# Two of the four weight sums of a column group, made by accumulating transfers from GpSimd's queue instead of VectorE adds

## The chip, the cores and the metric

The kernel runs on one core of a Trainium2 chip. The metric is the device time of one execution in microseconds (us). TensorE is called PE, VectorE DVE, ScalarE ACT, GpSimd POOL, and SyncE's queue, from which the kernel of before issues all its transfers, SP.

## What is computed

One decoder layer on a 1024 x 1024 float32 input: an RMSNorm, one input projection with a 1024 x 6144 weight, two token mixers side by side on its columns (retention with eight heads; a gated linear recurrence of width 1024), an output projection, the residual sum and a second RMSNorm.

```
xn = rms_norm(x, norm_in_g)
q, k, v, g_ret, x_lru, g_lru = split(xn @ w_in)           # six times 1024 columns
y_ret = group_norm(retention(rotary(q), rotary(k), v)) * silu(g_ret)
y_lru = rg_lru(conv(x_lru), gates) * silu(g_lru)
out   = rms_norm(x + concat(y_ret, y_lru) @ w_out, norm_out_g)
```

This case is about the product `xn @ w_in` for the 5120 columns other than v.

## The kernel before

**The product.** A float32 product is made of three products of rounded parts: a matrix is split into a high part (a cast on ACT, line 106) and a low part (a subtraction on DVE, line 107), and `mm3` (line 109) multiplies high by high, low by high and high by low. Above that stands a scheme with seven products in place of eight. The input is cut into four quarters (whose sums, P1 to P7, are made once, in the v stage, and kept), and so are 256 columns of the weight: `b11`, `b12` (upper 512 rows, first and second half of the columns), `b21`, `b22` (lower 512 rows). A **column group** (class `Quad`, line 383) is such a set of 256 columns; there are 20, here numbered 0 to 19. Groups 0 to 11 are the columns of x_lru, g_lru and g_ret, three groups for each pair of recurrence blocks; groups 12 to 19 are q and k, whose columns lie in the order (h j c) (`halves=True`).

**The sums of a group.** The seven products need four sums of weight quarters. `t13[:, 0]` is b11 + b12 (used by P5), `t13[:, 1]` is b12 + b22 (P7), `t24[:, 0]` is `t13[:, 0]` + b22 (P6) and `t24[:, 1]` is `t24[:, 0]` + b21 (P4). All four are DVE adds of 128 x 512 elements: lines 415, 434, 416 and 426. `t13` and `t24` are tiles of 128 x 1024 from the pool `sums`, which has two buffers; a third user is `graw`, the gate weights of a pair of recurrence blocks (line 628), once in three of the groups 0 to 11.

**The preparation of a group.** `load` (line 391) asks SP for the raw weight, two transfers of 512 KB. `prep1` splits b11 for P1 and makes `t13[:, 0]` and `t24[:, 0]`; `prep2` splits b21 and b22 (P2, P3) and makes `t24[:, 1]`; `prep3` splits `t24` (P6, P4) and makes `t13[:, 1]`; `prep4` splits `t13` (P5, P7). The split of `t24` and that of `t13` are an ACT cast and a DVE subtraction of 128 x 1024 each.

**What sets the order.** `Runner.step` (line 500) interleaves the products of one group with the preparation of the next and with pieces of the work behind the product (convolution, gates, scan, rotation), which are called fillers. A scheduler then places the instructions of each engine in a fixed order by dependences and its own costs; each engine runs its instructions strictly in that order, and one that waits holds up all that stand behind it on that engine. A tile takes the buffer of its pool that was released first. Twelve matmuls make one of the seven products of a group.

**Gates.** The recurrence's gates are matmuls with `gw` (line 591), the split form of `graw`. They stand between the products of the groups, and PE can't start them before `graw` has landed and been split.

Of the kernel before, what the change touches and what calls it, by code (L numbers as in the profile page):

```python
# [10 lines left out]
F32 = mybir.dt.float32  # L11
# [3 lines left out]
ALU = mybir.AluOpType  # L15

P = 128
# [23 lines left out]
def hybrid_layer(  # L41
# [17 lines left out]
    pe, act, dve, pool, sp = nc.tensor, nc.scalar, nc.vector, nc.gpsimd, nc.sync  # L59
# [3 lines left out]
    HALF = D // 2  # L63
# [3 lines left out]
    def pool_on(side, name, bufs):  # L67
        return tc.tile_pool(name=name, bufs=bufs, side=side, reuse_waits="tile")
# [36 lines left out]
    def split(src, hi, lo):  # L105
        act.copy(out=hi, in_=src)  # L106
        dve.tensor_tensor(out=lo, in0=src, in1=hi.bitcast(F32), op=ALU.subtract)  # L107
# [57 lines left out]
    sums = s_stack.enter_context(pool_on("right", "sums", 2))  # L165
# [83 lines left out]
    def v_phase():  # L249
        with pool_on("left", "vb", 6) as vb, pool_on("left", "vo", 10) as vo:  # L250
# [52 lines left out]
            for k in range(4):  # L303
                for t in range(4):
                    product("P1", A[t], t, True, False, [k])
            b21 = load(1, 0, vb, "bt")
            load_x("A12", xs_pool["P4"], "w", 1, 0)
            w_parts("P2", b21)
            x_parts("P2", xr["A12"])
            for t in range(4):  # L310
                snap("c11", t, A[t])
            load_x("A21", xs_pool["P4"], "w", 0, 1)
            b12 = load(0, 1, vb, "bt")
            load_x("A22", sums, "sum", 1, 1)
            b22 = load(1, 1, raw, "raw")

            combine(b11, b11, b12, ALU.add)
# [65 lines left out]
    class Quad:  # L383
# [7 lines left out]
        def load(self):  # L391
            r = raw.tile([P, 8, 256], F32, name="wraw", tag="raw")
            for kh in range(2):
                sp.dma_start(out=r[:, 4 * kh:4 * kh + 4],
                             in_=w_in[kh * HALF:(kh + 1) * HALF, self.col:self.col + 256]
                             .rearrange("(k p) c -> p k c", p=P))
            b = r.rearrange(self.order, kh=2, j=2, h=2)
            self.b = [[b[:, kh, :, j] for j in range(2)] for kh in range(2)]
            self.w = {}

        def pair(self):
            return [slabs.tile([P, 2, 4, 2, 64], F32R, name="wq", tag="w") for _ in range(2)]
# [5 lines left out]
        def prep1(self):  # L408
            (b11, b12), (b21, b22) = self.b
            s = slabs.tile([P, 2, 4, 2, 64], F32R, name="w11", tag="w")  # L410
            split(b11, s[:, 0], s[:, 1])
            self.put("P1", s[:, 0], s[:, 1])
            self.t24 = sums.tile([P, 2, 4, 2, 64], F32, name="t24", tag="sum")
            self.t13 = sums.tile([P, 2, 4, 2, 64], F32, name="t13", tag="sum")
            dve.tensor_tensor(out=self.t13[:, 0], in0=b11, in1=b12, op=ALU.add)
            dve.tensor_tensor(out=self.t24[:, 0], in0=self.t13[:, 0], in1=b22, op=ALU.add)

        def prep2(self):
# [9 lines left out]
        def prep3(self):  # L428
            (b11, b12), (b21, b22) = self.b
            h, l = self.pair()  # L430
            split(self.t24, h, l)
            self.put("P6", h[:, 0], l[:, 0])
            self.put("P4", h[:, 1], l[:, 1])
            dve.tensor_tensor(out=self.t13[:, 1], in0=b12, in1=b22, op=ALU.add)

        def prep4(self):
            h, l = self.pair()
# [257 lines left out]
    while run.i < len(run.q):  # L695
# [3 lines left out]
    op = {n: ctx.enter_context(pool_on("right", n, k)) for n, k in (  # L699
        ("qkc", 4), ("wraw", 3), ("wo", 10), ("yl", 16), ("vc", 4), ("h", 8))}  # L700
# [316 lines left out]
```

## Time and profile before

| | |
|---|---|
| median of 3 runs (lowest to highest) | 767.24 us (765.67 to 769.76) |
| the profiled execution: its own time, its span | 765.5 us, 763.7 us |
| PE busy, DVE busy, ACT busy, POOL busy | 734.1 us (96%), 548.6 us (72%), 413.4 us (54%), 0.2 us |
| granted TensorE clock, mean | 0.993 |
| stretch of the 20 column groups | from 89.7 us to 494.3 us of the span |

A row of the timeline gives the start and the length of an instruction in us, its engine and line, what it writes and reads, and in brackets how long its engine sat idle before it and what ended that. Consecutive instructions of an engine overlap a little, so the distance of two starts is less than a length. A matmul's row is longer than the distance to the next one, since matmuls are pipelined.

### The profile page before, as it was taken

Reading aid. Unit: us, or ns where it says so; the run is one execution under the profiler, and the core shown is the slowest. Engines: PE = TensorE matmul, PEld = TensorE weight load, DVE = VectorE, ACT = ScalarE, POOL = GpSimd, SP = SyncE. Lnnn points to the kernel's source line nnn. Section 1 sums busy time; section 2 is a strip of 40 time slices with the busy share of each in tenths; the row PEclk is TensorE's granted clock in tenths of the full one; section 3 lists DMA queues with packets and bytes.
Section 4 is the critical chain, followed back from the end, with each engine's and each line's share of the span. In section 5 each row is a group of like instructions: output and inputs, shape, how many; then the busy total and the mean of one; then the engine's idle time right before and its main releaser. Section 6 shows DMA issues by size and latency. Waiting matters only on the chain.

```text
span 763.7 us, 9411 instructions
## 1 busy us (share of the span) xinstructions
PE 734.1 (96%) x3508; PEld 610.8 (80%) x3508; DVE 548.6 (72%) x918; ACT 413.4 (54%) x635; POOL 0.2 (0%) x4
## 2 busy tenths in 40 slices
PE   6999999999999999999999999968999999899996
PEld 5877888887787788788788888757888898788885
DVE  6998647669977968977899888585567665652443
ACT  7784436695599679679533333255435443431332
POOL 0000000000000000000000000000000000000000
PEclk9999999999999999999999999999999999999999
DMA  9752712141214212421445542789946556331022
GB/s 317 268 191 88 245 53 70 56 128 38 72 52 161 74 55 87 148 83 52 169 122 126 134 110 56 226 266 323 313 146 206 194 179 235 97 129 36 28 88 106
DMA packets 85406, 105.58 MB, mean 138 GB/s; under 512 B 4848, under 2 KB 58224, under 8 KB 85360
## 3 DMA queue, kind: packets, MB, share of 16 engines
q1 hardware_dynamic: 85360, 104.99, 43.0%
q8 instruction: 27, 0.44, 0.2%
q14 instruction: 19, 0.16, 0.1%
HBM read 75.61 MB, written 29.36 MB: 137 GB/s over the span
## 4 chain that ended last, share of the span: by engine, by line
PE 67%; DVE 13%; ACT 10%; DMA 5%; issue 4%; SPq 0%; DVEq 0%; ACTq 0%
PE pp L112 59%; PE pp L826 2%; DVE xc L561 2%; PE pp L825 2%; PE pp L808 2%; PE pp L787 2%; DMA yraw<-l_d 2%; DVE wq L107 1%; ACT wq L106 1%; PE pp L847 1%; DVE y L614 1%; DVE wl L107 1%; DMA rot<-in_rot_t 1%; ACT L643 1%; PE pp L794 1%
## 5 line engine op out<-in xcount | busy, mean ns | idle before, releaser
L112 PE MATMUL pp<-wh,wq 128*128 128x512 f32 x960 | 301.6, 391 | 1.6 <-ACT cy L470 0.7
L112 PEld LDWEIGHTS pp<-wh,wq 128*128 128x128 f32 x960 | 179.9, 188 | 42.9 <-ACT cy L461 2.2
L112 PE MATMUL pp<-wo,yt 128*128 128x512 f32 (+1 forms) x792 | 186.1, 390 | 3.9 <-ACT yt L106 3.9
L112 PE MATMUL pp<-wl,wq 128*128 128x512 f32 x480 | 186.9, 389 | 0.0
L112 PEld LDWEIGHTS pp<-wo,yt 128*128 128x128 f32 x792 | 143.4, 189 | 31.6 <-ACT yt L106 4.3
L112 PEld LDWEIGHTS pp<-wl,wq 128*128 128x128 f32 x480 | 90.1, 188 | 18.5
L107 DVE TENSOR_TENSOR wq<-t,wq 128x1024 fp32r<-128x1024 f32 x40 | 48.7, 1221 | 39.1 <-ACT wq L106 32.1
L106 ACT CAST wq<-t 128x1024 fp32r<-128x1024 f32 x40 | 41.7, 1049 | 31.3 <-PE pp L112 26.7
L112 PE MATMUL pp<-wh 128*128 128x512 f32 x112 | 45.6, 407 | 8.0 <-ACT wh L106 8.0
L112 PE MATMUL pp<-wh,w 128*128 128x512 f32 x160 | 52.9, 391 | 0.1
L112 PE MATMUL pp<-wl,wh 128*128 128x512 f32 x112 | 44.8, 401 | 0.0
L112 PE MATMUL pp<-wh,wl 128*128 128x512 f32 x112 | 44.1, 398 | 0.0
L898 ACT ACTIVATE junk<-h 128x512 f32<-128x512 f32 (+1 forms) x17 | 10.3, 607 | 49.8 <-DVE h L914 25.3
L461 ACT COPY cy<-pp 128x512 f32<-128x512 f32 x20 | 11.6, 581 | 46.1 <-PE pp L112 45.5
L112 PEld LDWEIGHTS pp<-wh,w 128*128 128x128 f32 x160 | 30.0, 188 | 6.9 <-DVE w L107 0.6
L112 PEld LDWEIGHTS pp<-wh 128*128 128x128 f32 x112 | 21.8, 195 | 13.2 <-ACT wh L106 8.4
L112 PE MATMUL pp<-wl,w 128*128 128x512 f32 x80 | 31.1, 389 | 0.0
L839 ACT ACTIVATE yn<-pp,nb,rs_y 128x128 f32<-128x128 f32 x64 | 24.1, 458 | 11.8 <-DVE nb L837 11.8
L470 ACT COPY cy<-pp 128x512 f32<-128x512 f32 x20 | 11.6, 578 | 29.4 <-PE pp L112 29.3
L422 ACT CAST wq<-wraw 128x512 fp32r<-128x512 f32 x40 | 22.9, 617 | 8.3 <-PE pp L112 7.4
L97 ACT ACTIVATE rs_s<-ve 128x4 f32<-128x4 f32 x16 | 3.2, 202 | 43.8 <-DVE ve L832 43.8
L424 DVE TENSOR_TENSOR wq<-wraw,wq 128x512 fp32r<-128x512 f32 x40 | 26.7, 681 | 0.1
(154 smaller groups left out, 1116.2 us busy)
## 6 DMA issues: line engine op xcount, KB each, us to landing
wraw<-in_w_in SPq DMA_DIRECT2D x40, 512.0 KB, 4.7
qkc<-qk_d SPq DMA_DIRECT2D x16, 512.0 KB, 5.1
wor<-in_w_out SPq DMA_DIRECT2D x16, 512.0 KB, 5.7
bt<-in_w_in SPq DMA_DIRECT2D x20, 256.0 KB, 5.4
xA<-in_xT SPq DMA_DIRECT2D x16, 256.0 KB, 5.4
v_d<-vo SPq DMA_DIRECT2D x16, 256.0 KB, 2.4
xt<-in_x SPq DMA_DIRECT2D x8, 512.0 KB, 3.3
l_d<-y SPq DMA_DIRECT2D x8, 512.0 KB, 3.2
```

What stands on the lines that cost most here:

```text
L106: act.copy(out=hi, in_=src)
L107: dve.tensor_tensor(out=lo, in0=src, in1=hi.bitcast(F32), op=ALU.subtract)
L112: pe.matmul(ps, a, b, start=first and j == 0, stop=last and j == 2, skip_group_check=True)
L422: act.copy(out=h[:, j], in_=b)
L424: dve.tensor_tensor(out=l[:, j], in0=b, in1=h[:, j].bitcast(F32), op=ALU.subtract)
L461: act.copy(out=self.cy[:, :TH], in_=self.A)
L561: dve.scalar_tensor_tensor(out=xc[:, d:], in0=c[:, :T - d], scalar=cw[3 - d], in1=xc[:, d:], op0=ALU.mult, op1=ALU.add)
L787: heads(lambda h, hs: pe.matmul(psc[:, hs], k[:, hs], q[:, hs], start=True, stop=True))
L808: heads(lambda h, hs: pe.matmul(pkv[:, hs], kn[:, hs], vn[:, hs], start=True, stop=True))
L825: pe.matmul(po[:, hs], q[:, hs], st[:, h], start=True, stop=False)
L826: pe.matmul(po[:, hs], sm[:, h], vn[:, hs], start=st is None, stop=True)
L839: heads(lambda h, hs: act.activation(out=yn[:, hs], in_=po[:, hs], func=AF.Identity, scale=rs[:, h:h + 1], bias=nb[:, h:h + 1]))
```

## The change

`load` now also takes a buffer for `t13` and fills it by transfers. SP copies b11 into `t13[:, 0]` and b12 into `t13[:, 1]` straight from the weight in HBM (256 KB each; one transfer each in groups 0 to 11, two of 128 KB each in groups 12 to 19, where a row of 128 columns is two pieces of 64). Then POOL's queue issues transfers that read the weight again and add it to what stands in SBUF (`accum_op`): b12 onto `t13[:, 0]`, b22 onto `t13[:, 1]`. These are cut along k, so a group has four of 128 KB in groups 0 to 11 and eight of 64 KB in groups 12 to 19. A POOL transfer waits for SP's transfer into the same bytes, and DVE's add of `t24[:, 0]` (now line 431) waits for those of `t13[:, 0]`. The two DVE adds of `t13` are gone, 40 instructions in all. Nothing else is edited, but the scheduler orders all engines anew, and lines behind 416 move by 15 or 14: 426 is now 441, 424 is 439, 457 is 471, 471 is 485, 480 is 494, 543 is 557, 561 is 575, 613 is 627, 669 and 670 are 683 and 684, 678 and 679 are 692 and 693.

```diff
             self.b = [[b[:, kh, :, j] for j in range(2)] for kh in range(2)]
             self.w = {}
+            self.t13 = sums.tile([P, 2, 4, 2, 64], F32, name="t13", tag="sum")
+            for j, (kh0, kh1) in enumerate(((0, 0), (0, 1))):
+                for kh, jj, o in ((kh0, j, None), (kh1, 1, ALU.add)):
+                    src = w_in[kh * HALF:(kh + 1) * HALF, self.col:self.col + 256] \
+                        .rearrange(self.order.replace("p (kh k)", "(k p)").replace("kh ", ""), p=P, j=2, h=2)[:, :, jj]
+                    if self.order.endswith("(h j c) -> p kh k j h c"):
+                        for h in range(2):
+                            if o is None:
+                                sp.dma_start(out=self.t13[:, j, :, h], in_=src[:, :, h])
+                            else:
+                                for k in (0, 2):
+                                    pool.dma_start(out=self.t13[:, j, k:k + 2, h], in_=src[:, k:k + 2, h], accum_op=o)
+                    elif o is None:
+                        sp.dma_start(out=self.t13[:, j].rearrange("p k h c -> p k (h c)"), in_=src.rearrange("p k h c -> p k (h c)"))
+                    else:
+                        for k in (0, 2):
+                            pool.dma_start(out=self.t13[:, j, k:k + 2].rearrange("p k h c -> p k (h c)"), in_=src[:, k:k + 2].rearrange("p k h c -> p k (h c)"), accum_op=o)
...
             self.t24 = sums.tile([P, 2, 4, 2, 64], F32, name="t24", tag="sum")
-            self.t13 = sums.tile([P, 2, 4, 2, 64], F32, name="t13", tag="sum")
-            dve.tensor_tensor(out=self.t13[:, 0], in0=b11, in1=b12, op=ALU.add)
             dve.tensor_tensor(out=self.t24[:, 0], in0=self.t13[:, 0], in1=b22, op=ALU.add)
...
             self.put("P4", h[:, 1], l[:, 1])
-            dve.tensor_tensor(out=self.t13[:, 1], in0=b12, in1=b22, op=ALU.add)
```

**Which buffer `t13` takes.** In the program that results, `t13` of a group takes the buffer of the group before's `t24`, which DVE releases by its split of that `t24`; in groups 3, 6, 9 and 12, where `graw` took that one, it takes the buffer of the group before's `t13`.

**DVE, the preparation of group 4.** In these rows a tile's number tells its buffer. Before, `t24_1199` and `t13_1200` are group 3's, `t24_1358`, `t13_1359` and `w11_1355` are group 4's. Before, on DVE from group 3's split of `t24` to group 4's second add of `t24`:

```order
L107 TENSOR_TENSOR wq_1277<-t24_1199,wq_1276 128x1024
L415 TENSOR_TENSOR t13_1359<-wraw_1323 128x512
L434 TENSOR_TENSOR t13_1359<-wraw_1323 128x512
L543 TENSOR_TENSOR cx_1082<-cx_1082,rstd_b_71 128x1024
L480 TENSOR_TENSOR cy_1083<-pp_1203,cy_1083 128x512
L107 TENSOR_TENSOR wq_1318<-t13_1200,wq_1317 128x1024
L107 TENSOR_TENSOR w11_1355<-wraw_1323,w11_1355 128x512
L416 TENSOR_TENSOR t24_1358<-t13_1359,wraw_1323 128x512
L457 TENSOR_TENSOR cx_1260<-pp_1326,cx_1260 128x512
L426 TENSOR_TENSOR t24_1358<-t24_1358,wraw_1323 128x512
```

and now, where `t24_1218` and `t13_1177` are group 3's, `t13_1342`, `t24_1381` and `w11_1378` are group 4's:

```order
L107 TENSOR_TENSOR wq_1294<-t24_1218,wq_1293 128x1024
L485 TENSOR_TENSOR cy_1096<-pp_1220,cy_1096 128x512
L607 TENSOR_TENSOR y_1255<-y_1255,xc_1116 128x1024
L107 TENSOR_TENSOR wq_1334<-t13_1177,wq_1333 128x1024
L431 TENSOR_TENSOR t24_1381<-t13_1342,wraw_1339 128x512
L441 TENSOR_TENSOR t24_1381<-t24_1381,wraw_1339 128x512
L557 TENSOR_TENSOR cx_1095<-cx_1095,rstd_b_71 128x1024
L494 TENSOR_TENSOR cy_1096<-pp_1220,cy_1096 128x512
L107 TENSOR_TENSOR w11_1378<-wraw_1339,w11_1378 128x512
```

The add of line 431 needs the transfers into `t13_1342`, which may start when the split of `t24_1218` has released that buffer. The low part of P1's weight (`w11`), which stood ahead of the first add of `t24`, now stands four instructions behind it.

**PE, the gates between groups 3 to 5.** `gw` is the gates' weight, `xh` their input; `wh_429`, `wh_430`, `wl_431`, `wl_432` belong to P6. Before, from the first matmul of P6 of group 5 to the first gate:

```order
L112 MATMUL pp_1549<-wh_429,wq_1563 128x512
L112 MATMUL pp_1549<-wl_431,wq_1563 128x512
L112 MATMUL pp_1549<-wh_429,wq_1564 128x512
L112 MATMUL pp_1549<-wh_429,wq_1563 128x512
L112 MATMUL pp_1549<-wl_431,wq_1563 128x512
L112 MATMUL pp_1549<-wh_429,wq_1564 128x512
L112 MATMUL pp_1549<-wh_430,wq_1563 128x512
L112 MATMUL pp_1549<-wl_432,wq_1563 128x512
L112 MATMUL pp_1549<-wh_430,wq_1564 128x512
L112 MATMUL pp_1549<-wh_430,wq_1563 128x512
L112 MATMUL pp_1549<-wl_432,wq_1563 128x512
L112 MATMUL pp_1587<-xh_1517,gw_1544 128x512
```

and now, the same stretch:

```order
L112 MATMUL pp_1574<-wh_429,wq_1588 128x512
L112 MATMUL pp_1574<-wl_431,wq_1588 128x512
L112 MATMUL pp_1574<-wh_429,wq_1589 128x512
L112 MATMUL pp_1611<-xh_1542,gw_1569 128x512
```

The first gate stood behind eleven matmuls of P6 and now stands behind three. In the next pair of blocks (group 8) it stood behind eight matmuls of P6 and now stands behind one; in the last (group 11) behind one, and now behind three.

**DVE, a q/k group (18).** Before, from group 17's split of `t24` (`t24_3435`) to group 18's second add of `t24` (`t24_3569`; `t13_3570` and `w11_3566` are its own):

```order
L107 TENSOR_TENSOR wq_3498<-t24_3435,wq_3497 128x1024
L471 TENSOR_TENSOR cy_3348<-pp_3443,cy_3348 128x512
L415 TENSOR_TENSOR t13_3570<-wraw_3532 128x512
L434 TENSOR_TENSOR t13_3570<-wraw_3532 128x512
L107 TENSOR_TENSOR wq_3529<-t13_3436,wq_3528 128x1024
L416 TENSOR_TENSOR t24_3569<-t13_3570,wraw_3532 128x512
L107 TENSOR_TENSOR w11_3566<-wraw_3532,w11_3566 128x512
L426 TENSOR_TENSOR t24_3569<-t24_3569,wraw_3532 128x512
```

and now, where `t13_3509` and `t24_3556` are group 18's, from its line 431 to its split of `t13`:

```order
L431 TENSOR_TENSOR t24_3556<-t13_3509,wraw_3506 128x512
L692 TENSOR_TENSOR cx_3312<-cx_3312,rot_2954 128x1024
L692 TENSOR_TENSOR cy_3313<-cy_3313,rot_2954 128x1024
L693 TENSOR_TENSOR cx_3312<-cx_3312,t_3536 128x1024
L693 TENSOR_TENSOR cy_3313<-cy_3313,t_3537 128x1024
L439 TENSOR_TENSOR wq_3594<-wraw_3506,wq_3593 128x512
L441 TENSOR_TENSOR t24_3556<-t24_3556,wraw_3506 128x512
L107 TENSOR_TENSOR wq_3617<-t24_3556,wq_3616 128x1024
L485 TENSOR_TENSOR cy_3457<-pp_3562,cy_3457 128x512
L107 TENSOR_TENSOR wq_3647<-t13_3509,wq_3646 128x1024
```

Group 18's `w11` stands six instructions ahead of line 431 now. Between line 431 and the split of `t24`, which releases the buffer that group 19's `t13` waits for, stand four passes of the rotation (lines 692 and 693), a low part (439) and the second add (441).

## Rows read from the trace of the kernel before

**Rows 1.** The page: busy time of the engines, and the chain that ended last.

```profile
PE 734.1 (96%) x3508; PEld 610.8 (80%) x3508; DVE 548.6 (72%) x918; ACT 413.4 (54%) x635; POOL 0.2 (0%) x4
...
PE 67%; DVE 13%; ACT 10%; DMA 5%; issue 4%; SPq 0%; DVEq 0%; ACTq 0%
```

**Rows 2.** Windows, the column groups: length; PE, PEld, DVE, ACT, POOL busy; clock; DMA share; GB/s.

```profile
89.70:494.30 404.60, 401.53 (x1753) 327.21 (x1751) 325.20 (x364) 247.33 (x312) 0.00 (x0) 1.00 0.33 98
```

**Rows 3.** Groups of DVE instructions by form: busy us, mean ns | idle before.

```profile
L107 DVE TENSOR_TENSOR wq<-t,wq 128x1024 fp32r<-128x1024 f32 x40 | 48.7, 1221 | 39.1 <-ACT wq L106 32.1 <-PE pp L112 7.0
...
L415 DVE TENSOR_TENSOR t<-wraw 128x512 f32<-128x512 f32 x20 | 13.7, 686 | 1.8 <-DMA wraw<-in_w_in 1.5
...
L561 DVE SCALAR_TENSOR_TENSOR xc<-cy,par_sb,xc 128x1023 f32<-128x1023 f32 x4 | 5.1, 1278 | 1.8 <-ACT xc L568 1.8
```

**Rows 4.** The transfers: queue with packets, MB, share; issues with KB, median us to landing.

```profile
q1 hardware_dynamic: 85360, 104.99, 43.0%
...
yraw<-l_d SPq DMA_DIRECT2D x8, 512.0 KB, 6.3
...
graw<-in_gate_w SPq DMA_DIRECT2D x4, 256.0 KB, 3.0
...
ident<-in_ident_in SPq DMA_DIRECT2D x1, 64.0 KB, 1.9
```

**Rows 5.** Line 682, SP transfers of two pieces: issue ns, and landing, min/median/max.

```profile
L682 SPq DMA_DIRECT2D qk_d<-cy x16: 574/948/1477, 385.7 to 512.6; - x16
...
DMA to landing us min/median/max: 3.2/3.9/5.2
```

**Rows 6.** Timeline of DVE, preparation of group 4.

```profile
150.14 1.22 DVE L107 TENSOR_TENSOR wq<-t,wq 128x1024 fp32r<-128x1024 f32 x1
...
156.10 1.22 DVE L107 TENSOR_TENSOR wq<-t,wq 128x1024 fp32r<-128x1024 f32 x1
157.23 0.68 DVE L107 TENSOR_TENSOR w<-wraw,w 128x512 fp32r<-128x512 f32 x1
157.83 0.68 DVE L416 TENSOR_TENSOR t<-t,wraw 128x512 f32<-128x512 f32 x1
```

**Rows 7.** Timeline of PE, first matmul of group 4's P1.

```profile
163.45 0.39 PE L112 MATMUL pp<-wh,w 128*128 128x512 f32 x1
```

**Rows 8.** Timeline, group 5: its splits of t, SP's load of `graw`, first gate.

```profile
176.52 1.20 DVE L107 TENSOR_TENSOR wq<-t,wq 128x1024 fp32r<-128x1024 f32 x1
...
191.82 1.22 DVE L107 TENSOR_TENSOR wq<-t,wq 128x1024 fp32r<-128x1024 f32 x1
...
193.07 0.35 SPq L629 DMA_DIRECT2D graw<-in_gate_w  x1
...
198.31 0.50 PE L112 MATMUL pp<-xh,gw 128*128 128x512 f32 x1 [0.89 <-ACT gw L106]
```

**Rows 9.** Timeline of PE, first gates of the third and fourth pair of blocks.

```profile
261.64 0.50 PE L112 MATMUL pp<-xh,gw 128*128 128x512 f32 x1 [0.16 <-ACT gw L106]
...
323.70 0.50 PE L112 MATMUL pp<-xh,gw 128*128 128x512 f32 x1 [0.56 <-ACT gw L106]
```

**Rows 10.** Timeline, groups 10 and 13: split of t, first matmul of P1.

```profile
279.87 1.22 DVE L107 TENSOR_TENSOR wq<-t,wq 128x1024 fp32r<-128x1024 f32 x1
...
292.73 0.39 PE L112 MATMUL pp<-wh,w 128*128 128x512 f32 x1
...
343.14 1.22 DVE L107 TENSOR_TENSOR wq<-t,wq 128x1024 fp32r<-128x1024 f32 x1
...
356.53 0.39 PE L112 MATMUL pp<-wh,w 128*128 128x512 f32 x1
```

**Rows 11.** Timeline, q/k groups: a split of t24, two first matmuls of P1.

```profile
388.56 1.22 DVE L107 TENSOR_TENSOR wq<-t,wq 128x1024 fp32r<-128x1024 f32 x1 [0.52 <-ACT wq L106]
...
398.51 0.39 PE L112 MATMUL pp<-wh,w 128*128 128x512 f32 x1
...
417.55 0.39 PE L112 MATMUL pp<-wh,w 128*128 128x512 f32 x1
```

## The prediction, made before the changed kernel was run

> **What bounds the kernel now.** I read the page's busy times first and the chain second. PE is busy 96% of the span, and most of the chain that ended last is PE's own work [rows 1]. Then the windows view of the stretch that the change touches, the twenty column groups: PE is busy 401.5 of 404.6 us at the full granted clock, DVE 325 us, POOL nothing [rows 2]. So PE bounds these 404.6 us, and DVE, from which the change takes work, is idle for a fifth of them. All of PE's idle time there is 3.1 us; that is the most that any relief of DVE can give back, 0.4% of the time. It lies below 0.5%, which is about what a measurement of this kernel can tell from no change.
>
> The timelines give PE's pace: P1 of two q/k groups starts 19.04 us apart [rows 11], which for 84 matmuls is 0.227 us each, 2.72 us for a product of twelve. P6 comes four products behind its group's P1 (10.9 us), and needs the low part of its weight at its third matmul (0.45 us later). DVE's pace, start to start, is 1.13 us for 128x1024 and 0.60 for 128x512 [rows 6].
>
> **What is removed.** Forty adds, 0.686 us each [rows 3]: 27 us of DVE's time. Next to none of it is on the path, by the 3.1 us above. I count 1.0 us back, a third of PE's idle time: the gates' waits are counted below by themselves, and some short waits for low parts should go.
>
> **What is added: a chain of transfers.** Before, the sum `t13[:, 0]` cost one DVE add right after the raw weight. Now it begins when DVE's split of the `t24` of the group before releases the buffer (the front part says which), and passes through SP, POOL and DVE. The trace shows no transfer from POOL's queue and no accumulating one, so I bound each step.
> - SP's copy of b11, issue to landing: 3.0 us for 256 KB [rows 4], 3.9 for two-piece transfers with 3.2 and 5.2 as ends [rows 5]. I take 3.5, between the two kinds.
> - POOL's issues: two per sum in groups 0 to 11, four in groups 12 to 19. SP's issues of two-piece transfers take 0.57 to 1.48 us [rows 5]; I take 1.1, the upper half, since nothing says that POOL is as quick as SP.
> - The last landing: the smallest large transfer, 64 KB, lands in 1.9 us [rows 4]. A POOL transfer has 256 rows of 512 or 256 bytes, 16 for each of 16 engines, and the mean packet takes 43% x 16 x 763.7 us / 85,360 = 62 ns [rows 4], so 1.0 us more for reading and adding: 2.9. Its ends are 1.9 and 6.3, the slowest load of the trace [rows 4].
> - 0.3 us for the two hand-overs by semaphore, an estimate.
>
> Call the chain C. It is 3.5 + 2 x 1.1 + 2.9 + 0.3 = **9 us** in groups 0 to 11 and 3.5 + 4 x 1.1 + 2.9 + 0.3 = **11 us** in groups 12 to 19. Ends: 3.2 + 2 x 0.57 + 1.9 = 6 and 3.2 + 4 x 0.57 + 1.9 = 7.4 below, 5.2 + 2 x 1.48 + 6.3 = 14.5 and 5.2 + 4 x 1.48 + 6.3 = 17.4 above. Rows of SP's loads stand on either side of each step, and my values lie in the lower half since these transfers are small.
>
> The landing is the step that a page prices. By the Trainium skill, "DMA: Bandwidth & Descriptors", section "Anatomy of one DMA — SWDGE (gpsimd) path", a GpSimd transfer costs 2.0 us plus its bytes at 436 GB/s; 2.3 us for 128 KB is my estimate from it, which would shorten both chains by some 0.6 us and make the sum below about 3. No run here shows a GpSimd transfer yet.
>
> **Where the chain reaches PE.** In each place I set release + C + the DVE work behind it against the moment PE needs it. All times are of the profiled execution.
> - *Group 4.* Group 3's `t24` is split at 150.14 to 151.36 [rows 6]; `t13[:, 0]` is ready at 160.4. DVE then has line 431, 441, the multiply of 557, 494 and `w11` in order: 0.6 + 0.6 + 1.13 + 0.6 + 0.68 = 3.6, so `w11` is whole at 164.0. PE wants it at 163.45 + 0.45 = 163.9 [rows 7]. **+0.1**. Before, `w11` stood at 157.23 [rows 6]; six us of slack are gone, because it now stands behind the add that waits.
> - *Group 5 and its gates.* Group 4's `t24` is split by 177.72 [rows 8]; the sum is ready at 186.7. Line 431, three convolution taps of 1.2 (1.28 long [rows 3]), 439, 441 and 485 are 6.0, the split 1.2: it ends at 193.9. Before, it ended at 193.04, and SP's load of `graw`, which waits for that buffer, went at 193.07 [rows 8]. So `graw` comes 0.9 later, and the gates, moved eight matmuls (1.8 us) forward on PE, wait that much more on top of their 0.89 [rows 8]. **+2.7**.
> - *Gates of the next pairs.* Group 8's stand seven matmuls (1.6 us) earlier; DVE has one add of 0.6 less ahead: **+1.0** on their wait of 0.16 [rows 9]. Group 11's stand two matmuls later, which covers their wait of 0.56 [rows 9]: **-0.6**.
> - *Groups 10 and 13.* They repeat group 4: the splits end at 281.09 and 344.36 [rows 10], the sums are ready at 290.1 and 355.4. Behind them DVE has 3.6 and 3.0 us to `w11`: 293.7 and 358.4, where PE wants it at 293.2 and 357.0 [rows 10]. **+0.5** and **+1.4**. Group 7 is not late: DVE waits there for a root on ACT anyway.
> - *Groups 15 to 19.* Here the split of one group's `t24` releases the buffer for the next group's `t13`, so the chain is a loop. It takes C, line 431, four rotation passes of 1.13, 439, 441, ACT's cast and the split: 11 + 0.6 + 4.5 + 1.2 + 1.1 + 1.2 = 19.7 us, against PE's 19.04. It starts at 389.78 [rows 11]; group 15, with two passes, has its split done at 389.8 + 11 + 7.6 = 408.4, 1.4 ahead of PE's 398.51 + 10.9 + 0.45 = 409.85. Each of four groups loses 0.7 of it: **+1.2** at group 19.
> - *The others*, groups 0 to 3, 6, 9, 12 and 14, have other DVE work and several us between. I cost them nothing; if C is over 12 they are next.
>
> Sum: 0.1 + 2.7 + 1.0 - 0.6 + 0.5 + 1.4 + 1.2 - 1.0 = **+5.3 us**. The profiled execution took 765.5 us, so 770.8; the median of the runs shown is 1.74 above it, so **772.5**.
>
> **What I cost at nothing.** Traffic: 1 MB more per group in 19 us on queues that are busy a third of the stretch [rows 2]. SP: behind the copies stand the raw loads of the next group but one, wanted a step later. POOL: nothing else is in its queue. `t13[:, 1]`, whose transfers come second, is cast some 10 us later. Each of these covers is about 10 us.
>
> **The rivals.**
> - *The chain is hidden.* With C at 8 or below (10.3 in q/k), the loop is no slower than PE (19.04 - 8.7 = 10.3) and `w11` is in time everywhere. At 7 and 9: group 5's gates still lose 0.7, group 8's 1.0, against 0.6 and 1.0 of relief: **767**. At best all idle time goes: 764. For it: all its steps have lower ends that make it 6. Against: POOL would have to be about as quick as SP. This is the case that isn't slower; it decides at C = 8.
> - *POOL's issues are held by DVE.* If POOL can issue only between DVE's instructions, each issue waits for up to the 1.22 us of one [rows 3]: C = 9 + 2 x 1.22 = 11.4 and 11 + 4 x 1.22 = 15.9. The loop is then 24.6 us, 5.6 over PE's period, four times, after a first lateness of 3.4: 26. Groups 4, 5 and 10 add 2.4 each to their terms, group 13 adds 4.9: +2.5, +5.1, +2.9, +6.3. With the gates of groups 8 and 11 and the relief, +42: **809**. For it: DVE is busy 80% of the stretch [rows 2]. Against: where DVE already waits at line 431, nothing holds POOL. By the Trainium skill, "GPSIMD Engine Reference", section "Key points", GpSimd shares its interfaces to SBUF with VectorE, and they contend while a VectorE instruction reads two inputs from SBUF, as nearly every one here does; no run here shows it.
> - That the change doesn't do what it says is excluded by the order: 40 adds are gone from DVE.
>
> **How the numbers follow.** I give 0.36 to the hidden chain, 0.44 to my forecast, 0.20 to held or otherwise slow issues. Each us on both chains costs some 9 us beyond C = 9 (five loop groups and four others), so the forecast's own range, C from 8.3 to 11, is 769 to 790. The range goes from 764, the most that can be won, to 800, a chain of 12, and leaves out the upper part of the last case. Faster by over 0.5% (below 763.4) needs more than the idle time of the stretch: 0.06. Slower by over 0.5% (above 771.1) takes the slow case and all but the lower edge of mine: 0.62. The rest, 0.32, is no change that can be told.
>
> **What would show it.** Right: DVE idle ahead of line 431, ended by a transfer of POOL, most of it in groups 4, 10, 13 and 15 to 19; P1 starts of the last groups about 19.7 us apart; the gates of group 5 idle for 3 us or more; DVE's busy time down by 27 us with PE's unchanged. C is read from the end of a split of `t24` to the start of the next line 431. Wrong: P1 starts 19.04 apart and no waits at 431 (the first rival); issues on POOL that end with DVE's instructions and P1 starts 24 us apart (the second); or a stall on SP or at a cast of `t13`, which I count as covered.

## The result: 913 us in place of 768, and where the 145 us went

The changed kernel takes 913.18 us (911.57 to 914.23), the kernel before 768.5 (medians of four runs each): a ratio of 1.188, 95% interval 1.184 to 1.193. My prediction was 772.5, range 764 to 800. The direction was right, the size was wrong by a factor of nearly thirty (+145 for +5.3).

The page of the changed kernel: the span, the busy times, and the shares of the chain that ended last.

```profile
span 910.2 us, 9834 instructions
...
PE 774.0 (85%) x3508; PEld 635.4 (70%) x3508; DVE 526.4 (58%) x878; ACT 414.0 (45%) x636; POOL 136.7 (15%) x116
...
PE 33%; issue 23%; DVE 11%; DMA 8%; POOL 8%; ACT 5%; SPq 0%; DVEq 0%; POOLq 0%; ACTq 0%
```

PE's share of the chain falls from 67% [rows 1] to 33%. POOL, which did nothing before, now holds 8% itself, and 23% is "issue": an engine that stands still although the profile shows nothing that it waits for. DVE is relieved by 22 us (I had said 27), and it brings nothing.

Next, the same stretches in both: from the first P1 to that of group 12, and from there to that of group 19 (columns as in rows 2). The kernel before:

```profile
89.70:340.16 250.46, 248.22 (x1081) 201.52 (x1080) 199.55 (x223) 180.13 (x223) 0.00 (x0) 1.00 0.25 82
340.16:474.67 134.51, 134.11 (x589) 110.11 (x588) 114.41 (x130) 62.57 (x84) 0.00 (x0) 1.00 0.40 108
```

The changed kernel:

```profile
90.40:391.67 301.27, 263.40 (x1082) 210.91 (x1080) 187.66 (x201) 184.21 (x225) 60.86 (x50) 0.94 0.46 109
391.67:607.53 215.86, 153.59 (x590) 121.24 (x588) 100.21 (x109) 60.20 (x83) 65.17 (x54) 0.83 0.51 102
```

The first twelve groups lose 51 us, the seven steps through the q/k groups 81 (30.8 us per group in place of 19.2), the rest 14, at whose start group 19's second sum has still to land (at 627.5). The DMA engines are busy about half of the two stretches (0.46 and 0.51), so bandwidth is not used up.

PE loses in two ways. It is idle for 107 us more, and it runs the same 3,508 matmuls but is busy 40 us longer, since the granted clock, 1.00 in both stretches before, averages 0.94 and 0.83: after its new idle times PE works at the lower of its two levels (1.2 GHz in place of 2.4) for a while. The first matmul behind P1 of group 16 (it is group 15's P4) takes twice the 0.39 us of [rows 11]:

```profile
523.77 0.80 PE L112 MATMUL pp<-wh,wq 128*128 128x512 f32 x1 [12.06 <-ACT cy L484]
```

Why it had to wait 12 us stands in two rows of ACT: its cast of group 16's `t24`, and behind it its copy of group 15's P7 (line 484, 470 before) out of the sum that P4 adds onto next.

```profile
522.19 1.04 ACT L106 CAST wq<-t 128x1024 fp32r<-128x1024 f32 x1 [17.27 <-DVE t L441]
523.14 0.58 ACT L484 COPY cy<-pp 128x512 f32<-128x512 f32 x1
```

P7 was done before P1 began at 508.8, but its copy stands behind a cast that waits for a late sum. ACT had the same order before, in groups 17 to 19, where it cost nothing; for group 17:

```profile
436.61 1.05 ACT L106 CAST wq<-t 128x1024 fp32r<-128x1024 f32 x1 [4.67 <-PE pp L112]
437.57 0.58 ACT L470 COPY cy<-pp 128x512 f32<-128x512 f32 x1
```

PE's waits for line 484 behind such a cast are 40.9 us. Another 21.6 us are waits for DVE's subtraction of line 485, which also reads a sum that PE adds onto next, and stands behind a line 431 that waits for POOL. Together they are 62 of the 107 us.

What POOL does stands in its timeline (start, length, idle time before it). Three transfers of a q/k group:

```profile
446.69 1.21 POOL L411 DMA_DIRECT2D t<-in_w_in  x1 [7.75 <-issue]
450.07 1.23 POOL L411 DMA_DIRECT2D t<-in_w_in  x1 [2.16 <-issue]
453.48 1.21 POOL L411 DMA_DIRECT2D t<-in_w_in  x1 [2.19 <-issue]
```

And line 411, all 64 transfers of the q/k groups (issue ns min/median/max; idle us and times; landing):

```profile
L411 POOL DMA_DIRECT2D t<-in_w_in x64: 1203/1213/1229, 370.3 to 622.4; - x64
...
  issue: 172.3, 62
...
DMA to landing us min/median/max: 2.9/3.1/8.7
```

An issue takes 1.21 us whatever DVE does, but the starts stand 3.4 us apart (median). A transfer lands 3.1 us after its start (median; up to 8.7 while a load of SP is in flight, 3.9 at most without one), and the next starts 0.26 to 0.32 us after the landing: so for 100 of the 111 pairs of neighbours in the trace, all 63 of the q/k groups among them. No two of the 112 transfers are ever under way together. Eight a group make at least 27 us, where PE needs 19.

Two rows of DVE in the preparation of group 17 show whom this holds up: the split of group 16's `t13`, and line 431.

```profile
535.21 1.23 DVE L107 TENSOR_TENSOR wq<-t,wq 128x1024 fp32r<-128x1024 f32 x1 [10.12 <-ACT wq L106]
...
547.29 0.69 DVE L431 TENSOR_TENSOR t<-t,wraw 128x512 f32<-128x512 f32 x1 [6.18 <-DMA t<-in_w_in]
```

The first waits for a cast of group 16's second sum, whose last transfer landed at 533.7; the second for group 17's first sum, whose transfers could start only behind it, though their buffer was free at 524.5 and SP's copy there at 528.7.

### The profile page after: what moved, and what is told of

Same layout as the page of the kernel before. It is cut to its first block, busy times and chain, and to the rows that moved or that the text cites. A ratio compares the mean times of both kernels' runs of the same rounds, so it can differ in the third digit from the quotient of the medians.

```text
span 910.2 us, 9834 instructions
## 1 busy us (share of the span) xinstructions
PE 774.0 (85%) x3508; PEld 635.4 (70%) x3508; DVE 526.4 (58%) x878; ACT 414.0 (45%) x636; POOL 136.7 (15%) x116
## 3 DMA queue, kind: packets, MB, share of 16 engines
q1 hardware_dynamic: 114928, 115.48, 40.9%
q0 software_dynamic: 30464, 10.49, 10.9%
## 4 chain that ended last, share of the span: by engine, by line
PE 33%; issue 23%; DVE 11%; DMA 8%; POOL 8%; ACT 5%; SPq 0%; DVEq 0%; POOLq 0%; ACTq 0%
PE pp L112 26%; POOL t L411 6%; DMA t<-in_w_in 5%; POOL t L416 2%; PE pp L840 1%; DMA yraw<-l_d 1%; PE pp L839 1%; PE pp L822 1%; PE pp L801 1%; DVE wq L107 1%; DVE y L627 1%; DVE y L628 1%; DVE xc L575 1%; PE pp L861 1%; ACT wq L106 1%
## 5 line engine op out<-in xcount | busy, mean ns | idle before, releaser
L112 PE MATMUL pp<-wh,wq 128*128 128x512 f32 x960 | 322.9, 412 | 82.6 <-ACT cy L484 42.5
L112 PEld LDWEIGHTS pp<-wh,wq 128*128 128x128 f32 x960 | 191.6, 200 | 134.5 <-ACT cy L484 45.2
L112 PE MATMUL pp<-wl,wq 128*128 128x512 f32 x480 | 196.6, 410 | 0.0
L112 PEld LDWEIGHTS pp<-wl,wq 128*128 128x128 f32 x480 | 96.4, 201 | 20.5
L411 POOL DMA_DIRECT2D t<-in_w_in x64 | 77.9, 1217 | 185.1 <-issue 172.3
L416 POOL DMA_DIRECT2D t<-in_w_in x48 | 58.6, 1220 | 301.5 <-issue 109.8
L431 DVE TENSOR_TENSOR t<-t,wraw 128x512 f32<-128x512 f32 x20 | 13.8, 692 | 103.8 <-DMA t<-in_w_in 80.1
L112 PE MATMUL pp<-wh,w 128*128 128x512 f32 x160 | 56.4, 415 | 13.4 <-DVE w L107 13.1
L112 PEld LDWEIGHTS pp<-wh,w 128*128 128x128 f32 x160 | 32.0, 202 | 21.6 <-DVE w L107 14.0
L112 PE MATMUL pp<-xh,gw 128*128 128x512 f32 x64 | 24.2, 442 | 8.7 <-ACT gw L106 8.7
L853 ACT ACTIVATE yn<-pp,nb,rs_y 128x128 f32<-128x128 f32 x64 | 24.1, 458 | 11.8 <-DVE nb L851 11.8
```

The lines of the kernel that those rows point to most:

```text
L112: pe.matmul(ps, a, b, start=first and j == 0, stop=last and j == 2, skip_group_check=True)
L411: pool.dma_start(out=self.t13[:, j, k:k + 2, h], in_=src[:, k:k + 2, h], accum_op=o)
L416: pool.dma_start(out=self.t13[:, j, k:k + 2].rearrange("p k h c -> p k (h c)"), in_=src[:, k:k + 2].rearrange("p k h c -> p k (h c)"), acc ...
L853: heads(lambda h, hs: act.activation(out=yn[:, hs], in_=po[:, hs], func=AF.Identity, scale=rs[:, h:h + 1], bias=nb[:, h:h + 1]))
```

## The experiments

Why does POOL run one transfer at a time? The program has no wait between the two halves of a sum. Three theories: **A, room**: the launch of this kernel (both versions) keeps only 1,024 bytes of each SBUF partition for the descriptors of POOL's transfers (`dynamic_dma_scratch_size=1024`), and two halves don't fit. **B**: accumulating transfers wait for each other. **C**: POOL's queue runs any transfer alone.

**e1 and e2: three times the room.**

```diff
-    nc = bacc.Bacc("TRN2", target_bir_lowering=False, num_devices=1, dynamic_dma_scratch_size=1024)
+    nc = bacc.Bacc("TRN2", target_bir_lowering=False, num_devices=1, dynamic_dma_scratch_size=3072)
...
-        with pool_on("left", "vb", 6) as vb, pool_on("left", "vo", 10) as vo:
+        with pool_on("left", "vb", 6) as vb, pool_on("left", "vo", 9) as vo:
...
-    w4 = ph_stack.enter_context(pool_on("left", "w4", 10))
+    w4 = ph_stack.enter_context(pool_on("left", "w4", 9))
```

> The changed kernel with 3,072 bytes of each SBUF partition kept for POOL's transfer descriptors in place of 1,024 (two buffer pools, vo and w4, give up a buffer each for it, 10 to 9). In the changed kernel each POOL transfer starts 0.32 us after the one before has landed. Theory A (room): two halves of a sum don't fit into the space for descriptors, so they go one at a time; with three times the space the starts of a group's transfers stand 1.3 to 1.6 us apart in place of 3.4 to 3.9, a q/k group's eight take 12 us in place of 27 or more, and the time falls from 913 to some 5 to 20 us above the same kernel without the change (e2). Theory B (an accumulating transfer waits for the one before) and theory C (POOL's queue runs any transfer alone): the spacing stays 3.4 to 3.9, and the time 913 plus what e2 shows for the buffers.

> The kernel of before with the same 3,072 bytes and the same two pools cut from 10 to 9 buffers: the control for e1. No theory says anything of it; within 2% of before, 760 to 785, is likely, since a tenth of the buffers of two pools is gone.

e1 took 818.49 us, e2 798.88. The missing buffers alone cost 31 us (e2 to before 1.038, interval 1.034 to 1.043), more than the 760 to 785 expected; against e2 the change now costs 20 us, the upper end of what A expected. (e2 loses 28 of its 33 us of span between groups 4 and 15, so some of e1's chain may be hidden there.) POOL in e1:

```profile
451.36 6.18 POOL L411 DMA_DIRECT2D t<-in_w_in  x5 [8.14 <-DMA t<-in_w_in]
458.10 2.44 POOL L411 DMA_DIRECT2D t<-in_w_in  x2 [0.55 <-issue]
```

Five transfers go 0.73 us apart, closer than the 1.3 to 1.6 expected; the sixth at 458.10, 0.27 after the first has landed. Five is the most that are ever under way in e1. B and C fall, and the room can be estimated: five halves fit in 3,072 bytes, two don't in 1,024, so one takes between 512 and 614 bytes.

**e3: quarters, at 1,024 bytes.**

```diff
-                                for k in (0, 2):
-                                    pool.dma_start(out=self.t13[:, j, k:k + 2, h], in_=src[:, k:k + 2, h], accum_op=o)
+                                for k in range(4):
+                                    pool.dma_start(out=self.t13[:, j, k:k + 1, h], in_=src[:, k:k + 1, h], accum_op=o)
```

(and so in the other branch.)

> The changed kernel with each accumulating transfer cut in four along k in place of two: twice as many transfers with half the rows, the space for descriptors as it is. Theory A (room): a transfer takes half the space, so about three are under way at a time; starts come 1.3 us apart until the space is full, sixteen of a q/k group in some 22 us; time 800 to 850. Theories B and C (one at a time): each still takes about 3 + 0.3 us, so a q/k group takes 16 x 3.3 = 53 us in place of 33 and a group before it 8 x 3.3 = 26 us: over 1,050 us.

811.8 us: with twice as many transfers the kernel takes 101 us less. Three are under way at most, and their starts stand 0.9 us apart (median):

```profile
462.62 4.46 POOL L411 DMA_DIRECT2D t<-in_w_in  x5 [3.01 <-issue]
```

**e4 and e8: copies**, halves as in the changed kernel and uncut; the accumulation is left out (`accum_op=o` is dropped).

> The changed kernel with POOL's transfers as plain copies: the accumulation is left out, so t13 holds b12 and b22 in place of the two sums; sizes, order and waits are the same. Theory A (room): a copy doesn't read what stands in its target and should need half the descriptors, so several fit: starts 1.3 us apart, time 765 to 785. Theory B (accumulating): the same, 1.3 us apart, 765 to 785. Theory C (any transfer alone): 3.3 to 3.9 us apart and about 905. That DVE holds the issues (my second rival) would show as issue lengths that vary with DVE's work; in the changed kernel all are 1.20 to 1.33 us.

> As e4 (copies, accumulation left out), but not cut along k: one transfer of 256 KB in place of two of 128 KB, two of 128 KB in place of four in q/k groups. Theory A (room): such a copy has as many rows as two halves and takes over half the space, as an accumulating half does, so the next is issued only 0.3 us after it has landed, at 3 us or more from start to start, although nothing accumulates. Theory B (only accumulating transfers go one at a time): starts 0.7 us apart as in e4.

e4 took 782.91 us, e8 789.69. In e4 three are under way at most:

```profile
375.33 2.15 POOL L411 DMA_DIRECT2D t<-in_w_in  x3 [14.76 <-DVE y L627]
381.60 1.45 POOL L411 DMA_DIRECT2D t<-in_w_in  x2 [4.11 <-issue]
```

In e8 never more than one, with nothing that accumulates:

```profile
447.92 0.75 POOL L410 DMA_DIRECT2D t<-in_w_in  x1 [5.06 <-issue]
450.98 0.75 POOL L410 DMA_DIRECT2D t<-in_w_in  x1 [2.30 <-issue]
```

So it is the room that a transfer takes: an accumulating half and a copy of twice its rows each take more than half of the 1,024 bytes, a copy of as many rows at most a third.

**e5 and e6: the second sum alone by transfers**, in halves and in quarters.

```diff
             for j, (kh0, kh1) in enumerate(((0, 0), (0, 1))):
+                if j == 0: continue
...
+            dve.tensor_tensor(out=self.t13[:, 0], in0=b11, in1=b12, op=ALU.add)
             dve.tensor_tensor(out=self.t24[:, 0], in0=self.t13[:, 0], in1=b22, op=ALU.add)
```

> The changed kernel with t13[:, 0] made by DVE again and only t13[:, 1] by transfers: two halves per group, four in a q/k group. Theory A (POOL's transfers go one at a time for want of room, and the first sum's chain is what DVE waits for): line 431 waits for no transfer; the second sum is there 3.0 + 0.6 + 2 x 3.9 = 11.4 us after its buffer comes free in the first groups and 3.3 + 0.6 + 4 x 3.4 = 17.5 us in q/k groups, against some 18 that the split of t13 leaves it: 766 to 785, nearly all of the 145 us back. Rival (the loss lies in the new order of the engines or in t13's early buffer, not in the first sum's chain): well over 800.

> As e5, with each accumulating transfer cut in four along k, since the quarters of e3 went 0.9 us apart. Theory A: the second sum is there 3.0 + 0.6 + 3 x 0.9 + 2.5 = 9 us after its buffer in the first groups and 3.3 + 0.6 + 7 x 0.9 + 2.5 = 13 us in q/k groups, so nothing waits for it: 765 to 770, no difference from before; 20 adds less on DVE buy nothing, PE having had 3.1 us of idle time. Rival (relief of DVE pays): under 763.

e5: 775.71 us (ratio 1.010, 1.007 to 1.013); ACT's casts of `t13` wait four times for transfers, 16 us in all, so the 18 us are too tight in places; that the 8 us come from there is likely, not shown. e6: 768.67 against 767.85 (1.001, 0.999 to 1.003), no difference: half of the change can be had at no cost, and for no gain.

**e7: no POOL transfers** (the `pool.dma_start` lines are dropped, so the second operands are left out).

> The changed kernel without POOL's transfers: the second operand of both sums is left out, t13 holds b11 and b12. Buffers, SP's copies and what the scheduler makes of it stay near the changed kernel's. Theory A (the loss is POOL's queue): the chain is SP's 3 us alone, 765 to 772. Rival (early buffer, SP's copies and the order cost by themselves): 785 or more.

765.05 us, ratio 0.9966 (0.9948 to 0.9985). This is about what taking 40 adds from DVE is worth when the sums come for nothing: 2.6 us by the ratio (1.2 to 4.0; 2.8 by the medians), where PE's idle time had allowed 3.1 [rows 2]. The early buffers, SP's copies and the new order cost nothing by themselves.

**e9 and e10: the first sum alone by transfers**, in halves and in quarters; `t13[:, 1]` is DVE's add in `prep3` again.

> The changed kernel with t13[:, 1] made by DVE again and only t13[:, 0] by transfers: two halves per group, four in a q/k group, one at a time. POOL's queue then has 4 x 3.4 = 14 us of work in a q/k group of 19 and is no longer full, so only the chain C is left: 3.0 + 0.6 + 3.9 + 3.5 + 0.2 = 11.2 us in the first groups, 3.3 + 0.6 + 3 x 3.4 + 3.1 + 0.2 = 17.4 us in q/k groups. With my prediction's own terms (the loop is C + 8.7 = 26.1 against 19.04, four times, after a first lateness of 4.9; groups 4, 5, 10 and 13 pay 2.3, 4.9, 2.7 and 7.8; gates +0.4, relief -1) that is +50: 818. So of the 145 us, some 50 would be the chain's length and some 95 the full queue, in which the second sum's transfers of one group hold up the first sum's of the next. Rival (the second sum plays no part): 890 or more.

> As e9, with each accumulating transfer cut in four, 0.9 us apart: C is 3.0 + 0.6 + 3 x 0.9 + 2.5 + 0.2 = 9.0 us in the first groups, the value of my prediction, and 3.3 + 0.6 + 7 x 0.9 + 2.5 + 0.2 = 12.9 in q/k groups (11 in the prediction). By the prediction's terms: loop 21.6, 2.6 over, four times, first lateness 0.4; group 13 pays 3.3; the rest 2.7: +17, 784. If the terms were too small, it comes out well above 790; if slack hides the chain, at 770 or less.

e9 took 864.47 us (1.127, 1.116 to 1.137), 98 above before, where 50 were expected. e10 took 807.36 (1.052, 1.045 to 1.060), 41 above before, where 17 were expected. Both expectations missed, in the same direction. In e10 C was 8.6 to 10 us in six of the first groups, about as expected, but 11 to 15 in groups 1, 5, 6, 8 and 11, and 11.8 to 15.4 in q/k. In groups 1, 5 and 8 SP's copy landed after 4 to 5 us in place of 3, with raw loads in flight; in group 6 it went 4.6 us after its buffer was free. What PE waited for in e10 (us, times, longest):

```profile
PE pp L112 <- ACT cy L486: 11.6, 5, 5.0
PE pp L112 <- ACT gw L106: 8.5, 3, 3.5
PE pp L112 <- DVE cy L487: 6.9, 3, 3.1
```

The gates alone wait for 8.5 us, against 1.6 before [rows 8, 9]. Of the first row 10.9 us, and all of the last, are the waits shown above: for ACT's copy behind a cast of `t24`, and for DVE's subtraction behind the add that waits for POOL (lines 486 and 487 here). That is 17.8 us, and with 6.9 more at the gates nearly all of PE's new idle time of 25.0 us. The other 15.7 us of e10's longer span (804.4 against 763.7) are PE's longer busy time for the same matmuls: 749.8 against 734.1, at a mean granted clock of 0.973 against 0.993.

The 145 us, each run against the median of before beside it: 41 for the first sum's chain with transfers that overlap (e10), 3 more for the second sum's (e3), and 100 because no two are under way together (the change). The steps hang together: with the first sum alone, overlap is worth 57 us (e9 to e10).

## Why the prediction was wrong, step by step

- *PE bounds the stretch, and DVE's relief is worth 3.1 us at most*: right; e7 got 2.6 of it. PE's busy time, which I had said would stay, rose by 40 us with the lower clock.
- *SP's copy, 3.5 us*: right, 3.3 in the first groups and 3.1 in q/k (medians). *The landing, 2.9*: nearly, 3.5 in the first groups and 3.1 in q/k. *The hand-overs, 0.3*: three, and 0.85 together in group 4 (0.03 from DVE to SP, 0.64 from SP to POOL, 0.18 from POOL to DVE).
- ***POOL's issues, 1.1 us each* is the step that failed.** The issue itself takes 1.21. But I bounded it by SP's rows [rows 5], and so took the length of one issue for the distance of two starts. That distance is landing plus 0.32: 3.9 and 3.4 us. C came out at 11 to 12 us in most of the first groups and at 16 to 26 in q/k, past my upper end of 17.4 in six of the eight. With room for five (e1) it was 8.0 to 8.8 in most of the first groups and 9.6 to 12 in q/k, around the 9 and 11 that I had.
- *"POOL: nothing else is in its queue"* and the cover of 10 us for `t13[:, 1]` fell with it. At 3.4 us or more, a q/k group's eight transfers fill the queue for longer than the group lasts, so each group's second sum came 16 to 20 us after its first and held up the next group's first. I had costed both at nothing without multiplying a count by a price. The change against e9, each above its own before, puts 46 us on it.
- *Where the chain reaches PE* is a second step that failed: the terms were too small even where C was about mine, +20 in e1 (against e2) for my +5, +41 in e10 for +17. I let PE need the split of `t24` at its own group's P6, 10.9 us behind P1. In groups 16 to 19 PE stops at the product right behind P1, 2.7 us after its start, since ACT's copy stands behind the cast of `t24`: 8.2 us less slack than I had counted. My terms followed the order of DVE and PE, not ACT's. The gates' wait grew by 6.9 us, not 3.1, and I had taken one landing time for SP's copy in all groups.
- *The clock* has no term in my sum. It is 15.7 of e10's 40.7 us, and 40 of the change's 146 us of span.
- Two slips are too small to matter: two matmuls cover 0.45 us of a wait, not 0.6, and with a landing 0.6 us shorter my own terms give 2.3 us, not 3.
- *The rivals.* That DVE holds POOL's issues is refuted: all 112 took 1.20 to 1.33 us, 100 of 111 started 0.26 to 0.32 us after a landing, and landings hardly follow DVE's work (correlation with its busy share -0.2 in the first groups and 0.3 in q/k, both without the transfers that met a load of SP). The contention that the Trainium skill states ("GPSIMD Engine Reference", section "Key points") is not seen in these lengths. That rival's number, 809, has nothing to do with the true cause, and that it lies near e3's time is chance. That the chain is hidden was refuted by the result. The right rival was missing: how many of POOL's transfers can be under way at once. The number that decides it stood in the kernel's launch, which I had not weighed.

## What to carry to other kernels

Before work goes to a queue that a trace has never shown busy, ask for three numbers: the time of one transfer, how many can be under way together, and how many a stage issues; the time that the stage's transfers take by these three, against the stage's period (here, one at a time, 8 x 3.4 = 27 us against 19), comes before any question of latency. If a queue's starts stand a landing apart and the profile puts its idle time down to "issue", look for the room that its transfers need: cut them smaller or give them more, and weigh what that room takes from other buffers (31 us here). To find how much slack a late result has, read the order of every engine that waits for it: what stands behind the wait is late too, whether it needs the result or not. And an add on an engine that doesn't bound the stage is worth PE's idle time, no more: 2.6 us for forty.

## What the runs showed of the hardware

- POOL's queue needs room in SBUF for each transfer under way. The most seen with 1,024 bytes of a partition: one accumulating transfer of 256 rows (the change), three of 128 rows (e3), three copies of 256 rows (e4), or one copy of 512 (e8). With 3,072: five accumulating ones of 256 (e1). When the room is used up, POOL stands still and starts the next about 0.3 us after the oldest has landed (0.32 in the change, 0.27 in e1). The Trainium skill, "DMA: Bandwidth & Descriptors", section "SWDGE vs HWDGE vs iDMA", says that GpSimd's descriptors stand in rings in a piece of SBUF; these runs agree, and show the price when the piece is small.
- An issue takes 1.21 us for an accumulating transfer of 256 rows, and 0.72 for a copy of as many (e4); alone, an accumulating transfer lands after 3.1 (64 KB) and 3.5 us (128 KB), and a copy, with others under way, after 2.3 and 2.7 (medians). With room for five, accumulating transfers start 0.73 us apart (e1), so the 1.21 us are not what an issue keeps the next one waiting. The estimate of 2.3 us for 128 KB that the prediction gives by the Trainium skill, "DMA: Bandwidth & Descriptors", section "Anatomy of one DMA — SWDGE (gpsimd) path", was 0.4 short for copies and 1.2 for accumulating transfers.
